# Rotating the SSM state on VectorE ahead of its output matmul

## The chip, the core and the metric

One core of a Trainium2 chip runs the whole program: one launch, all inputs and the output in HBM. The metric is the device time of one execution in microseconds (us). Three executions of the kernel before gave 2878.36, 2879.96 and 2882.97 us; their median, 2879.96 us, is the time before.

## The reference, cut to what matters

The program is one block of a trunk: 16 meta tokens and 2048 tokens of width 1024 pass through a token mixer (a state space model beside an mLSTM, each with its gate) and a gated feed-forward part. The change lies in the state space model (SSM) alone. It has 32 groups of 16 channels, and each group has 64 complex states. With real and imaginary parts written apart, the reference computes for each group

```python
bu_re = jnp.einsum('blgh,gph->blgp', u, bb_re)
bu_im = jnp.einsum('blgh,gph->blgp', u, bb_im)
_, _, x_re, x_im = lax.associative_scan(_complex_affine_combine, (a_re, a_im, bu_re, bu_im), axis=1)
y = (jnp.einsum('blgp,ghp->blgh', x_re, c_re) - jnp.einsum('blgp,ghp->blgh', x_im, c_im) + d * u)
```

that is, a linear recurrence x[t] = a x[t-1] + B u[t] with complex a, and the output y = Re(C x) + d u. The sequence is 2064 tokens long.

## The kernel before, in words

**The SSM by chunks of eight tokens.** The kernel cuts the 2064 tokens into 258 chunks of 8 (the 258 columns of most of its tiles; `C8` in the code). For one group, the inputs of a chunk (8 tokens by 16 channels) stand on the 128 partitions of a tile `ug`, one column per chunk. A first matmul with the weights `wi` gives `vp`: what a chunk adds to the state, 64 real parts on the upper partitions and 64 imaginary parts on the lower ones. Between chunks the state would be multiplied by a complex number a^8. The kernel turns the state by its angle instead, so that the recurrence becomes real: it multiplies `vp` by a rotation (cosines `cc`, sines `ss`, made per group on VectorE from small tables `et`), scans with the real factor `R8` (one `tensor_tensor_scan`, giving `xr`, the state in the turned frame), and has to turn the result back. The output of a group then has three parts, summed in one accumulator `yp` in PSUM: the direct response within a chunk, `tt` times `ug`, and the response to the state at the chunk's start.

**How the turning back is done before.** The turned-back state would be `xr*cc` minus the half-swapped `xr` times `ss` (imaginary and real halves changed over). The kernel never forms that. It forms `xc = xr*cc` (L418) and `xs = xr*ss` (L419) on VectorE, and gives each a matmul with its own weights: `w1` for `xc` (L422) and `w2` for `xs` (L423), where `w2` has the halves changed over and the sign already in it. Both weights are made once, in a stage ahead: for each of 8 blocks of four groups a loop (L797) runs `comb` twice, three VectorE operations each (L790, L791, L792), over a `W1` buffer of which there is one, and writes the result to scratch in HBM (`wo1_d` and `wo2_d`, L800). `load_blk` reads them back for a block of four groups (L378).

**What runs beside it.** All inputs of TensorE here are fp32. The dense projections of the block are matmuls that are split into three products of a rounded part and a rest (L156, L157, L158, 410 columns each, 8 x 3 of them for one tile of a projection). VectorE takes each finished tile out of PSUM (`ev`, L351), ScalarE applies a tanh to it (L352), SyncE sends it to HBM (`gab_d`, `o_d`). There are two buffers of the kind `mm` in PSUM for these tiles, four of the kind `ac`, which the SSM uses. In the SSM's stage ScalarE also copies `vp` into `vs` with its halves changed over (L405, L406), and copies `yp` to `yo` (L425), which goes to HBM.

**What sets the order.** The code is written in stages: projections for the SSM, its preparation, the SSM, then the gates' projections, and so on. A scheduler reorders all of it before the program is built: it goes by priorities in the order of writing, but takes any instruction that its own timing model holds to be ready. So the gates' projections, written after the SSM, are laid between its instructions. What comes out is one fixed list for each engine; on the chip every engine works its list in order and waits at an instruction until what it needs is there. An edit in the SSM can therefore move instructions anywhere after it.

Of the kernel before, what the change touches and what calls it, by code (L numbers as in the profile page):

```python
# [9 lines left out]
F32 = mybir.dt.float32  # L10
F32R = mybir.dt.float32r
I32 = mybir.dt.int32
AF = mybir.ActivationFunctionType
ALU = mybir.AluOpType
# [12 lines left out]
C8 = 258  # L27
# [22 lines left out]
def mixer_ffn_kernel(  # L50
# [7 lines left out]
    stop=None,  # L58
):
    nc = tc.nc  # L60
    S, V, G, P, T = nc.scalar, nc.vector, nc.gpsimd, nc.sync, nc.tensor
# [9 lines left out]
    dp = pool(ctx, "scratch", space=DRAM)  # L71
# [12 lines left out]
    win_d = dp.tile([8, 128, 512], F32, name="win_d")  # L84
    tt_d = dp.tile([8, 128, 512], F32, name="tt_d")
    wo1_d = dp.tile([8, 128, 512], F32, name="wo1_d")
    wo2_d = dp.tile([8, 128, 512], F32, name="wo2_d")
    e_d = dp.tile([8, 128, 4 * 66], F32, name="e_d")

    const = pool(ctx, "const")  # L90
# [279 lines left out]
    def ssm(pl):  # L370
        def load_blk(blk):
            wi = pl.tile([128, 4, 128], F32, tag="wi", name="wi")
            tt = pl.tile([128, 4, 128], F32, tag="tt", name="tt")
            w1 = pl.tile([128, 4, 128], F32, tag="w1", name="w1")
            w2 = pl.tile([128, 4, 128], F32, tag="w2", name="w2")
            et = pl.tile([128, 4, 66], F32, tag="et", name="et", bufs=2)
            for dst, src in ((wi, win_d), (tt, tt_d), (w1, wo1_d), (w2, wo2_d)):
                P.dma_start(out=dst.rearrange("p g c -> p (g c)"), in_=src[blk])  # L378
            P.dma_start(out=et.rearrange("p g a -> p (g a)"), in_=e_d[blk])
            ug = pl.tile([128, 4, C8], F32, tag="ug", name="ug", bufs=2)  # L380
            P.dma_start(out=ug, in_=u_d[blk * 4:blk * 4 + 4].rearrange("g j h c -> (j h) g c"))
            return wi, tt, w1, w2, et, ug

        nxt = load_blk(0)
        for blk in range(8):
            wi, tt, w1, w2, et, ug = nxt
            for g in range(4):
                cc = pl.tile([128, 17, 16], F32, tag="cc", name="cc", bufs=2)
                ss = pl.tile([128, 17, 16], F32, tag="ss", name="ss", bufs=2)
                tb = pl.tile([128, 17, 16], F32, tag="tb", name="tb")  # L390
                shp = [128, 17, 16]
                e2 = lambda o: et[:, g, o:o + 16].unsqueeze(1).to_broadcast(shp)
                e1 = lambda o: et[:, g, o + 16:o + 33].unsqueeze(2).to_broadcast(shp)
                V.tensor_tensor(cc, e1(0), e2(0), ALU.mult)
                V.tensor_tensor(tb, e1(33), e2(33), ALU.mult)
                V.tensor_tensor(cc, cc, tb, ALU.subtract)
                V.tensor_tensor(ss, e1(33), e2(0), ALU.mult)
                V.tensor_tensor(tb, e1(0), e2(33), ALU.mult)
                V.tensor_tensor(ss, ss, tb, ALU.add)
                ccf = cc.rearrange("p a b -> p (a b)")  # L400
                ssf = ss.rearrange("p a b -> p (a b)")
                vp = pst("ac", [128, C8])
                T.matmul(out=vp, lhsT=wi[:, g, :], rhs=ug[:, g, :])
                vs = pl.tile([128, C8], F32, tag="vs", name="vs")
                S.activation(vs[0:64], vp[64:128], AF.Copy)  # L405
                S.activation(vs[64:128], vp[0:64], AF.Copy)  # L406
                a1 = pl.tile([128, C8], F32, tag="a1", name="a1", bufs=2)
                V.tensor_tensor(a1, vp, ccf[:, :C8], ALU.mult)
                V.tensor_tensor(vs, vs, ssf[:, :C8], ALU.mult)
                V.tensor_tensor(a1, a1, vs, ALU.add)  # L410
                xr = pl.tile([128, C8], F32, tag="xr", name="xr")
                V.tensor_tensor_scan(xr, R8[:, blk * 4 + g:blk * 4 + g + 1].to_broadcast([128, C8]), a1, 0.0,
                                     ALU.mult, ALU.add)
                xc = pl.tile([128, C8], F32, tag="xc", name="xc", bufs=2)
                xs = pl.tile([128, C8], F32, tag="xs", name="xs", bufs=2)
                V.memset(xc[:, 0:1], 0.0)
                V.memset(xs[:, 0:1], 0.0)
                V.tensor_tensor(xc[:, 1:C8], xr[:, 0:C8 - 1], ccf[:, 0:C8 - 1], ALU.mult)  # L418
                V.tensor_tensor(xs[:, 1:C8], xr[:, 0:C8 - 1], ssf[:, 0:C8 - 1], ALU.mult)  # L419
                yp = pst("ac", [128, C8])  # L420
                T.matmul(out=yp, lhsT=tt[:, g, :], rhs=ug[:, g, :], start=True, stop=False)
                T.matmul(out=yp, lhsT=w1[:, g, :], rhs=xc, start=False, stop=False)  # L422
                T.matmul(out=yp, lhsT=w2[:, g, :], rhs=xs, start=False, stop=True)  # L423
                yo = pl.tile([128, C8], F32, tag="yo", name="yo", bufs=3)
                S.activation(yo, yp, AF.Copy)  # L425
                P.dma_start(out=ys_d[blk * 4 + g].rearrange("h j c -> (h j) c"), in_=yo)
            if blk < 7:
                nxt = load_blk(blk + 1)
# [121 lines left out]
    with ExitStack() as phG:  # L550
# [52 lines left out]
        for h in range(4):  # L603
# [12 lines left out]
                 rhs=r2f[:, 0:2].rearrange("p a c -> p (a c)"))  # L616
# [29 lines left out]
    with ExitStack() as phS:  # L646
# [12 lines left out]
        nsg = sp.tile([128, 1], F32, name="nsg")  # L659
# [58 lines left out]
        sw = pool(phS, "sprep2")  # L718
# [32 lines left out]
        def big(nm, tag):  # L751
            return sw.tile([128, 32, 16], F32, tag=tag, name=nm)
# [8 lines left out]
        w1 = big("w1", "x2")  # L761
        V.tensor_tensor(bs, Bs, bc(zre), ALU.mult)
        V.tensor_tensor(w1, Bt, bc(zim), ALU.mult)
        V.tensor_tensor(bs, bs, w1, ALU.subtract)
        CA, CA2 = big("CA", "x0"), big("CA2", "x1")
        V.tensor_scalar(CA, Ct, sg, None, ALU.mult)
        V.tensor_scalar(CA2, Cs, nsg, None, ALU.mult)

        shf = sw.tile([128, 240], F32, name="shf")
        V.memset(shf, 0.0)  # L770
# [7 lines left out]
        for blk in range(8):  # L778
# [3 lines left out]
            def pw(a, j0):  # L782
                return a[:, gs, j0:j0 + 8].unsqueeze(3).to_broadcast(shp)

            def col(a):
                return a[:, gs, :].unsqueeze(2).to_broadcast(shp)

            def comb(dst, pa, ca, pb, cb, eng):
                tmp = sw.tile(shp, F32, tag="cmb", name="cmb")
                eng.tensor_tensor(dst, pa, ca, ALU.mult)  # L790
                eng.tensor_tensor(tmp, pb, cb, ALU.mult)  # L791
                eng.tensor_tensor(dst, dst, tmp, ALU.subtract)  # L792

            WB = sw.tile(shp, F32, tag="WB", name="WB")
            comb(WB, pw(Pcr, 0), col(bb), pw(Psr, 0), col(bs), V)
            for ca, cb, dst in ((CA, Cs, wo1_d), (CA2, Ct, wo2_d)):

                W1 = sw.tile([128, 4, 16, 8], F32, tag="W1", name="W1")
                comb(W1.rearrange("p g h j -> p g j h"), pw(Pc, 1), col(ca), pw(Ps, 1), col(cb), V)
                P.dma_start(out=dst[blk], in_=W1.rearrange("p g h j -> p (g h j)"))  # L800
            tpw = pst("tp", [128, 4, 128])
            kp = pst("ac", [128, 4, 16])
            for g in range(4):
# [570 lines left out]
```

## Time and profile before

| quantity | value |
|---|---|
| median of three executions | 2879.96 us |
| the profiled execution | 2886.44 us, of which the span from first to last instruction is 2884.7 us |
| TensorE granted clock | 0.99 of full speed |
| TensorE matmuls, busy | 2794.8 us, 97% of the span |
| TensorE weight loads, busy | 2506.7 us, 87% |
| VectorE (DVE), busy | 1798.8 us, 62% |
| ScalarE (ACT), busy | 1047.4 us, 36% |

In the profile PE is TensorE's matmuls, PEld its weight loads, DVE is VectorE, ACT ScalarE, POOL GpSimd and SP SyncE, which issues the DMAs. A row of a grouped view reads: line, engine, operation, output and inputs, shape, how often; then the busy time in us with the mean of one in ns; then the idle time of the engine ahead of such instructions and what ended it. A row of a view by stretches reads: the stretch, its length, and for each engine its busy time with its number of instructions; then the granted clock and the DMA's share. A row of the timeline reads: start in us, duration in us, engine, line, operation. One fp32 matmul is two instructions in the trace. The weights of the SSM are prepared from about 240 to 320 us of the span, and the SSM itself runs from about 320 to 492 us.

### The profile page before, as it was taken

How to read it: one execution, taken by the hardware profiler on the slowest of the kernel's cores; microseconds unless marked ns; L12 is line 12 of the kernel's file. 1: busy time of each engine (PE TensorE's matmuls, PEld its weight loads, DVE VectorE, ACT ScalarE, POOL GpSimd, SP SyncE). 2: the span in 40 equal slices, each digit the busy share in tenths (PEclk: the TensorE clock that was granted, in tenths of full speed). 3: DMA queues.
4: the chain of work that ended last, by engine and by line, in shares of the span. 5: the costliest groups of instructions: out<-in, count | busy, mean ns of one | idle time of the engine just before them, and what ended most of it. 6: DMA issues, size and time to landing. Idle time of an engine off the chain costs nothing.

```text
span 2884.7 us, 41374 instructions
## 1 busy us (share of the span) xinstructions
PE 2794.8 (97%) x15654; PEld 2506.7 (87%) x15654; DVE 1798.8 (62%) x3508; ACT 1047.4 (36%) x1995; POOL 183.2 (6%) x257
## 2 busy tenths in 40 slices
PE   8999999999999999998779999998999999999999
PEld 8999999999999987776579999996888888888887
DVE  4638897377555465576777777788777774224333
ACT  6102233233443444434344444444444443223221
POOL 1000000000000000212310000001000000000000
PEclk9999999999999999999989999999999999999999
DMA  8334453211454564676746222224222235334553
GB/s 303 105 73 137 169 162 117 74 69 70 147 158 134 159 200 134 196 221 219 234 142 201 80 81 84 71 82 175 81 84 78 87 98 179 95 99 146 166 168 125
DMA packets 328442, 389.74 MB, mean 135 GB/s; under 512 B 41569, under 2 KB 230390, under 8 KB 328114
## 3 DMA queue, kind: packets, MB, share of 16 engines
q1 hardware_dynamic: 328242, 387.10, 41.9%
q8 instruction: 123, 2.02, 0.3%
q14 instruction: 77, 0.63, 0.1%
HBM read 282.90 MB, written 104.12 MB: 134 GB/s over the span
## 4 chain that ended last, share of the span: by engine, by line
PE 83%; DMA 7%; DVE 6%; issue 2%; ACT 1%; POOL 1%; SPq 0%; POOLq 0%; DVEq 0%; ACTq 0%
PE mm L158 9%; PE mm L156 9%; PE mm L157 9%; PE ac L157 8%; PE ac L158 8%; PE ac L156 8%; PE ac L162 5%; PE ac L163 5%; PE ac L161 5%; PE mm L163 4%; PE mm L162 4%; PE mm L161 4%; DMA mk<-h_d 1%; DMA wo_d<-W 1%; DMA h_d<-mk 1%
## 5 line engine op out<-in xcount | busy, mean ns | idle before, releaser
L158 PE MATMUL mm<-hTh,wl 128*128 128x410 f32 (+3 forms) x1216 | 430.4, 354 | 0.0
L156 PE MATMUL mm<-hTh,wh 128*128 128x410 f32 (+3 forms) x1216 | 429.4, 353 | 0.1
L157 PE MATMUL mm<-hTl,wh 128*128 128x410 f32 (+3 forms) x1216 | 427.2, 351 | 0.0
L1275 DVE TENSOR_TENSOR yhl<-ys,yhl 128x1024 fp32r<-128x1024 f32 (+1 forms) x96 | 109.1, 1137 | 293.7 <-ACT yhl L1274 293.7
L157 PE MATMUL ac<-t,yhl 128*128 128x512 f32 x704 | 278.5, 396 | 0.0
L158 PE MATMUL ac<-t,yhl 128*128 128x512 f32 x704 | 277.3, 394 | 0.0
L156 PE MATMUL ac<-t,yhl 128*128 128x512 f32 x704 | 276.6, 393 | 0.0
L161 PE MATMUL mm<-t,w 128*128 128x258 f32 (+2 forms) x792 | 254.6, 322 | 12.6 <-ACT w L1142 9.7
L161 PE MATMUL ac<-t,w 128*128 128x258 f32 (+2 forms) x792 | 255.0, 322 | 12.1 <-ACT t L1047 8.0
L162 PE MATMUL mm<-t,w 128*128 128x258 f32 (+2 forms) x792 | 255.1, 322 | 1.3 <-DVE t L1048 1.3
L162 PE MATMUL ac<-t,w 128*128 128x258 f32 (+2 forms) x792 | 254.9, 322 | 1.1 <-DVE t L1048 1.1
L163 PE MATMUL mm<-t,w 128*128 128x258 f32 (+2 forms) x792 | 253.6, 322 | 1.7 <-DVE w L1143 1.7
L163 PE MATMUL ac<-t,w 128*128 128x258 f32 (+2 forms) x792 | 254.7, 322 | 0.0
L140 ACT ACTIVATE wh<-ws 128x512 fp32r<-128x512 f32 (+1 forms) x176 | 124.5, 708 | 317.7 <-PE mm L157 139.3
L156 PEld LDWEIGHTS mm<-hTh,wh 128*128 128x128 f32 x1216 | 229.2, 188 | 3.2 <-DVE ev L351 0.8
L157 PEld LDWEIGHTS mm<-hTl,wh 128*128 128x128 f32 x1216 | 229.2, 189 | 2.6
L158 PEld LDWEIGHTS mm<-hTh,wl 128*128 128x128 f32 x1216 | 229.2, 189 | 2.4
L1274 ACT ACTIVATE yhl<-ys 128x1024 fp32r<-128x1024 f32 (+1 forms) x96 | 94.8, 988 | 350.6 <-PE ac L157 349.0
L1142 ACT ACTIVATE w<-s 128x512 fp32r<-128x512 f32 x176 | 110.3, 630 | 192.5 <-PE ac L163 112.3
L161 PEld LDWEIGHTS mm<-t,w 128*128 128x128 f32 x792 | 151.0, 191 | 25.6 <-ACT w L1142 9.9
L161 PEld LDWEIGHTS ac<-t,w 128*128 128x128 f32 x792 | 150.7, 190 | 25.1 <-ACT t L1047 8.3
L142 DVE TENSOR_TENSOR wl<-ws,wh 128x512 fp32r<-128x512 f32 (+1 forms) x112 | 104.5, 936 | 108.4 <-ACT wh L140 108.1
(448 smaller groups left out, 6180.2 us busy)
## 6 DMA issues: line engine op xcount, KB each, us to landing
ys<-y_d SPq DMA_DIRECT2D x64, 512.0 KB, 3.7
wg<-in_w_gate_dram SPq DMA_DIRECT2D x44, 512.0 KB, 4.8
wu<-in_w_up_dram SPq DMA_DIRECT2D x44, 512.0 KB, 3.9
gab_d<-ev SPq DMA_DIRECT2D x80, 205.0 KB, 2.2
ws<-in_w_m_dram SPq DMA_DIRECT2D x32, 512.0 KB, 4.0
ws<-in_w_out_dram SPq DMA_DIRECT2D x64, 256.0 KB, 3.0
gat<-gab_d SPq DMA_DIRECT2D x48, 256.0 KB, 3.6
ys<-y_d SPq DMA_DIRECT2D x32, 384.0 KB, 3.1
```

The source lines that it names most:

```text
L140: S.activation(wh, ws, AF.Copy, scale=scale)
L142: V.tensor_tensor(wl, ws, wh.bitcast(F32), ALU.subtract)
L156: T.matmul(out=ps, lhsT=lh, rhs=rh, start=first, stop=False)
L157: T.matmul(out=ps, lhsT=lh, rhs=rl, start=False, stop=False)
L158: T.matmul(out=ps, lhsT=ll, rhs=rh, start=False, stop=last)
L161: T.matmul(out=ps, lhsT=lh, rhs=rh, start=first, stop=False, skip_group_check=True)
L162: T.matmul(out=ps, lhsT=lh, rhs=rl, start=False, stop=False, skip_group_check=True)
L163: T.matmul(out=ps, lhsT=ll, rhs=rh, start=False, stop=last, skip_group_check=True)
L1142: S.activation(t[:, 0], src, AF.Copy)
L1274: S.activation(yh, ys, AF.Copy)
L1275: V.tensor_tensor(yl, ys, yh.bitcast(F32), ALU.subtract)
```

## The change

VectorE forms the turned-back state, and one matmul takes it. `xs` becomes the half-swapped `xr`, copied by ScalarE in two instructions of 64 partitions each; VectorE multiplies it by `ss` in place, and subtracts it from `xc` in place. The matmul with `w2` goes, and with it everything that made and carried `w2`: `CA2`, the second `comb` of each block, the scratch `wo2_d`, its write and its read, and the `memset` of the first column of `xs`. The line numbers of the changed kernel differ by up to 3 from the ones before.

```diff
-            for dst, src in ((wi, win_d), (tt, tt_d), (w1, wo1_d), (w2, wo2_d)):
+            for dst, src in ((wi, win_d), (tt, tt_d), (w1, wo1_d)):
...
                 V.memset(xc[:, 0:1], 0.0)
-                V.memset(xs[:, 0:1], 0.0)
                 V.tensor_tensor(xc[:, 1:C8], xr[:, 0:C8 - 1], ccf[:, 0:C8 - 1], ALU.mult)
-                V.tensor_tensor(xs[:, 1:C8], xr[:, 0:C8 - 1], ssf[:, 0:C8 - 1], ALU.mult)
+                S.activation(xs[0:64, 1:C8], xr[64:128, 0:C8 - 1], AF.Copy)
+                S.activation(xs[64:128, 1:C8], xr[0:64, 0:C8 - 1], AF.Copy)
+                V.tensor_tensor(xs[:, 1:C8], xs[:, 1:C8], ssf[:, 0:C8 - 1], ALU.mult)
+                V.tensor_tensor(xc[:, 1:C8], xc[:, 1:C8], xs[:, 1:C8], ALU.subtract)
                 yp = pst("ac", [128, C8])
                 T.matmul(out=yp, lhsT=tt[:, g, :], rhs=ug[:, g, :], start=True, stop=False)
-                T.matmul(out=yp, lhsT=w1[:, g, :], rhs=xc, start=False, stop=False)
-                T.matmul(out=yp, lhsT=w2[:, g, :], rhs=xs, start=False, stop=True)
+                T.matmul(out=yp, lhsT=w1[:, g, :], rhs=xc, start=False, stop=True)
...
-        V.tensor_scalar(CA2, Cs, nsg, None, ALU.mult)
...
-            for ca, cb, dst in ((CA, Cs, wo1_d), (CA2, Ct, wo2_d)):
-
-                W1 = sw.tile([128, 4, 16, 8], F32, tag="W1", name="W1")
-                comb(W1.rearrange("p g h j -> p g j h"), pw(Pc, 1), col(ca), pw(Ps, 1), col(cb), V)
-                P.dma_start(out=dst[blk], in_=W1.rearrange("p g h j -> p (g h j)"))
+
+            W1 = sw.tile([128, 4, 16, 8], F32, tag="W1", name="W1")
+            comb(W1.rearrange("p g h j -> p g j h"), pw(Pc, 1), col(CA), pw(Ps, 1), col(Cs), V)
+            P.dma_start(out=wo1_d[blk], in_=W1.rearrange("p g h j -> p (g h j)"))
```

Since the scheduler lays all engines' lists anew, the change moves more than it edits. Two places in the built order show it. On VectorE, in the middle of the SSM, before (one group from its scan, L412, to the next group's start; `xc` is L418, `xs` L419, `cc`, `ss` and `tb` make the next group's rotation, `ev` takes a projection tile out of PSUM):

```order
L412 SCALAR_TENSOR_TENSOR xr<-R_2223,a_3416 128x258
L399 TENSOR_TENSOR ss<-ss,tb 128x272
L351 TENSOR_TENSOR ev<-mm,rb 128x410
L418 TENSOR_TENSOR xc<-xr,cc 128x257
L419 TENSOR_TENSOR xs<-xr,ss 128x257
L395 TENSOR_TENSOR tb<-et 128x272
```

and the same place with the change (the scan is now L410, `xc` L415, the product with the swapped half L418, the difference L419):

```order
L410 SCALAR_TENSOR_TENSOR xr<-R_2222,a_3371 128x258
L397 TENSOR_TENSOR ss<-ss,tb 128x272
L350 TENSOR_TENSOR ev<-mm,rb 128x410
L415 TENSOR_TENSOR xc<-xr,cc 128x257
L393 TENSOR_TENSOR tb<-et 128x272
L418 TENSOR_TENSOR xs<-xs,ss 128x257
L392 TENSOR_TENSOR cc<-et 128x272
L419 TENSOR_TENSOR xc<-xc,xs 128x257
```

Four instructions stand between the scan and the product that needs ScalarE's copies, where before the second use of `xr` followed the first at once. Over all 32 groups this number is three or more in 29, and 2, 1 and 2 in the others.

On TensorE, around a group's output matmuls in the same stretch (L156 to L158 are a gate's projection), before:

```order
L156 MATMUL mm<-hTh,wh 128x410
L422 MATMUL ac<-xc,w_3326 128x258
L423 MATMUL ac<-xs,w_3327 128x258
L157 MATMUL mm<-hTl,wh 128x410
L158 MATMUL mm<-hTh,wl 128x410
```

and with the change (the projection is L155 to L157 there):

```order
L157 MATMUL mm<-hTh,wl 128x410
L422 MATMUL ac<-xc,w_3281 128x258
L155 MATMUL mm<-hTh,wh 128x410
L156 MATMUL mm<-hTl,wh 128x410
L157 MATMUL mm<-hTh,wl 128x410
```

The second matmul is gone, and the scheduler spreads the groups wider: from the first group's `vp` matmul to the last one's there are 542 projection matmuls before and 695 with the change. In the stage ahead, from the first block's transposes to the last block's matmuls, there are 269 before and 205 with the change, since that stage has become shorter in the scheduler's model. The lists also differ again far behind, where the feed-forward part begins (about 1480 to 1600 us of the span): there the same instructions stand in a slightly different order.

More of the change, by code (lines that the diff above doesn't have):

```diff
@@ L86, in mixer_ffn_kernel @@
     wo1_d = dp.tile([8, 128, 512], F32, name="wo1_d")
-    wo2_d = dp.tile([8, 128, 512], F32, name="wo2_d")
     e_d = dp.tile([8, 128, 4 * 66], F32, name="e_d")
@@ L374, in load_blk @@
             w1 = pl.tile([128, 4, 128], F32, tag="w1", name="w1")
-            w2 = pl.tile([128, 4, 128], F32, tag="w2", name="w2")
             et = pl.tile([128, 4, 66], F32, tag="et", name="et", bufs=2)
-            for dst, src in ((wi, win_d), (tt, tt_d), (w1, wo1_d), (w2, wo2_d)):
+            for dst, src in ((wi, win_d), (tt, tt_d), (w1, wo1_d)):
                 P.dma_start(out=dst.rearrange("p g c -> p (g c)"), in_=src[blk])
@@ L381, in load_blk @@
             P.dma_start(out=ug, in_=u_d[blk * 4:blk * 4 + 4].rearrange("g j h c -> (j h) g c"))
-            return wi, tt, w1, w2, et, ug
+            return wi, tt, w1, et, ug
         nxt = load_blk(0)
         for blk in range(8):
-            wi, tt, w1, w2, et, ug = nxt
+            wi, tt, w1, et, ug = nxt
             for g in range(4):
@@ L764, in mixer_ffn_kernel @@
         V.tensor_tensor(bs, bs, w1, ALU.subtract)
-        CA, CA2 = big("CA", "x0"), big("CA2", "x1")
+        CA = big("CA", "x0")
         V.tensor_scalar(CA, Ct, sg, None, ALU.mult)
-        V.tensor_scalar(CA2, Cs, nsg, None, ALU.mult)
         shf = sw.tile([128, 240], F32, name="shf")
```

## The prediction

> **What bounds the kernel now.** I read the chain of waits first, then the waits of TensorE, then a view by stretches around the SSM, then the groups of instructions of its steady part.
>
> ```profile
> PE 83%; DMA 7%; DVE 6%; issue 2%; ACT 1%; POOL 1%; SPq 0%; POOLq 0%; DVEq 0%; ACTq 0%
> 240.00:320.00 80.00, 75.41 (x466) 72.33 (x465) 66.58 (x93) 19.16 (x40) 0.00 (x0) 1.00 0.44 158
> 340.00:480.00 140.00, 140.00 (x714) 133.30 (x713) 138.89 (x411) 48.22 (x110) 0.00 (x0) 1.00 0.50 152
> 504.00:576.00 72.00, 72.00 (x385) 71.60 (x385) 25.75 (x39) 15.68 (x24) 1.47 (x5) 1.00 0.21 69
> ```
>
> The chain that ends last is TensorE's for 83%. The columns of the other rows are PE, PEld, DVE, ACT, POOL. In the SSM's steady part (340 to 480 us) TensorE never idles at full clock, and VectorE is full too, 138.89 of 140 us. Just behind the SSM (504 to 576) TensorE is still full, while VectorE has two thirds of its time free: the projections go on. So the SSM runs in the background of a full TensorE, and what leaves TensorE's list there leaves the time. Only in the preparation (240 to 320) does TensorE idle, 80 - 75.41 = 4.6 us, by these waits:
>
> ```profile
> PE tp L805 <- DVE WB L792: 2.6, 2, 1.6
> PE ac L819 <- DVE ks L812: 1.4, 2, 0.9
> PE tp L805 <- ACT ev L352: 0.5, 1, 0.5
> ```
>
> They add up to 4.5 us, 4.0 of it VectorE being late.
>
> **What a removed matmul is worth.** 32 matmuls with `w2` go, two instructions each.
>
> ```profile
> L158 PE MATMUL mm<-hTh,wl 128*128 128x410 f32 x163 | 62.0, 380 | 0.0
> L156 PE MATMUL mm<-hTh,wh 128*128 128x410 f32 x164 | 61.2, 373 | 0.0
> L157 PE MATMUL mm<-hTl,wh 128*128 128x410 f32 x163 | 60.5, 371 | 0.0
> L423 PE MATMUL ac<-xs,w 128*128 128x258 f32 x56 | 16.7, 380 | 0.0
> ...
> 397.63 0.37 PEld L422 LDWEIGHTS ac<-xc,w 128*128 128x128 f32 x2
> 398.03 0.41 PEld L421 LDWEIGHTS ac<-ug,tt 128*128 128x128 f32 x2
> 398.46 0.41 PEld L423 LDWEIGHTS ac<-xs,w 128*128 128x128 f32 x2
> 398.89 0.19 PEld L158 LDWEIGHTS mm<-hTh,wl 128*128 128x128 f32 x1
> ...
> L423 PEld LDWEIGHTS ac<-xs,w 128*128 128x128 f32 x56 | 10.6, 189 | 1.4
> ```
>
> The mean of one instruction, 380 ns, is not its price. 64 x 0.380 would be 24.3 us, but the busy times of these groups (three projection rows, and four SSM matmuls of 16.7 us each) sum to 250 us in a stretch of 140: the instructions overlap. The price is the step from one to the next. The fence shows it for one group: 398.03, 398.46, 398.89, so 0.43 us for a matmul of two instructions. Over the stretch: 163 + 164 + 163 = 490 projection instructions and 4 x 56 = 224 of the SSM make 714, as the row by stretches says. Behind the SSM 385 instructions, nearly all projections, fill 72 us, 0.187 us each. So 140 - 490 x 0.187 = 48.4 us for 224, 0.216 us each. Removing 64 takes **13.8 us** from TensorE.
>
> The Trainium skill, "Perfetto Trace Analysis", section "Identifying the Most-Contended Engine", says that matmul busy time misleads because matmuls are pipelined, and that weight-load busy time is the better measure. The trace agrees on the first half. By the weight loads (one of these lasts 189 ns in the grouped view, and 64 of them 12.1 us) the sum would be 1.7 us smaller, and the forecast that much later; the measured steps decide for 13.8.
>
> **The preparation.** One `comb` of three operations goes from each of 8 blocks, with `CA2`:
>
> ```profile
> L792 DVE TENSOR_TENSOR W<-W,cmb 128x512 f32<-128x512 f32 x16 | 18.8, 1174 | 0.3
> L790 DVE TENSOR_TENSOR W<-Pc,CA 128x512 f32<-128x512 f32 x16 | 18.3, 1145 | 8.3 <-DMA wo_d<-W 8.3
> L791 DVE TENSOR_TENSOR cmb<-Ps,Ct 128x512 f32<-128x512 f32 x8 | 5.5, 690 | 0.2
> L767 DVE TENSOR_SCALAR CA<-Cs,nsg 128x512 f32<-128x512 f32 x1 | 0.5, 483 | 0.0
> ```
>
> 8 x (1.174 + 1.145 + 0.690) + 0.5 = 24.6 us of VectorE's work goes, and most of the 8.3 us that it waited for the one `W1` buffer to be written out, because that buffer is now used once per block and not twice. VectorE is what made TensorE late here. The gain lies between 0 (TensorE's list there has 64 projection matmuls fewer, so the stage is tighter for it too) and the whole 4.6 us. I take **3.5 us**, nearer the upper end, because 4.0 of the 4.5 us waited for VectorE, which loses a third of its 66.58 us. The 16 DMAs of 256 KB that go were beside other work, and I give them nothing.
>
> **The SSM on VectorE and ScalarE.** Here the change adds. Per group VectorE gains one tensor operation and loses a memset; ScalarE gains two copies; and a new wait arises, VectorE's product on ScalarE's copies.
>
> ```profile
> L412 DVE TENSOR_TENSOR_SCAN xr<-R,a 128x258 f32<-128x258 f32 x28 | 19.4, 692 | 0.1
> L351 DVE TENSOR_TENSOR ev<-mm,rb 128x410 f32<-128x410 f32 x21 | 12.2, 579 | 0.0
> L419 DVE TENSOR_TENSOR xs<-xr,ss 128x257 f32<-128x257 f32 x28 | 11.8, 423 | 0.0
> L142 DVE TENSOR_TENSOR wl<-ws,wh 128x1024 fp32r<-128x1024 f32 x5 | 6.1, 1221 | 0.0
> ...
> 399.29 0.42 DVE L409 TENSOR_TENSOR vs<-vs,ss 128x258 f32<-128x258 f32 x1
> 399.63 0.44 DVE L397 TENSOR_TENSOR ss<-et 128x272 f32<-128x272 f32 x1
> 399.99 0.44 DVE L396 TENSOR_TENSOR cc<-cc,tb 128x272 f32<-128x272 f32 x1
> 401.04 0.69 DVE L412 TENSOR_TENSOR_SCAN xr<-R,a 128x258 f32<-128x258 f32 x1
> 401.65 0.42 DVE L399 TENSOR_TENSOR ss<-ss,tb 128x272 f32<-128x272 f32 x1
> 401.98 0.58 DVE L351 TENSOR_TENSOR ev<-mm,rb 128x410 f32<-128x410 f32 x1
> 402.48 0.42 DVE L418 TENSOR_TENSOR xc<-xr,cc 128x257 f32<-128x257 f32 x1
> 406.29 0.60 PE L422 MATMUL ac<-xc,w 128*128 128x258 f32 x2
> ```
>
> VectorE's operations overlap too: the steps are about 0.345 us for a tensor operation (399.29, 399.63, 399.99), 0.61 for the scan, 0.50 for `ev`. A group before is 11 tensor operations, the scan, and its share of `ev` (21 in 28 groups) and of the weights' split L142 (5 in 28, about 1.15 each): 3.80 + 0.61 + 0.38 + 0.21 = 5.0 us. The trace has 28 groups in 140 us, 5.0 each. So VectorE, not TensorE alone, paces the groups now. With the change a group is 12 tensor operations, and the built order has 29 `ev` and 5 splits in 31 groups: 4.14 + 0.61 + 0.47 + 0.19 = 5.4 us, 167 us for 31 groups. TensorE's list between the same two points has 695 projection matmuls and 92 of the SSM with two instructions each: 695 x 0.187 + 184 x 0.216 = 170 us. VectorE still fits under TensorE, by some **2.6 us** in the whole stage, if it never waits. If it falls behind, the projections wait too, since `ev` stands in the same list and there are two `mm` buffers; and the matmul with `xc` waits. Before, that matmul came 406.29 - 402.90 = 3.4 us after its `xc` was done, and I take that for the slack with the change as well. Together 6.0 us of lateness cost TensorE nothing.
>
> The Trainium skill, "VectorE: DVE Perf Modes", section "The DRAIN you can't avoid", says that the next operation does not start until the pipe is empty. By it the added operation would cost its whole 423 ns, 31 x 0.08 = 2.4 us more in the stage, and the 2.6 us would be gone, though TensorE would still not wait. The trace differs: 0.34 us from start to start at 0.42 us each, and the same page says that an operation which nothing holds starts earlier.
>
> Does VectorE wait for the copies? The copies from SBUF are not in the trace of before. The nearest rows:
>
> ```profile
> L406 ACT ACTIVATE vs<-ac 64x258 f32<-64x258 f32 x28 | 10.6, 379 | 0.3
> L352 ACT ACTIVATE ev<-ev 128x410 f32<-128x410 f32 x21 | 11.5, 547 | 34.9 <-DVE ev L351 34.7
> L140 ACT ACTIVATE wh<-ws 128x1024 fp32r<-128x1024 f32 x5 | 5.3, 1062 | 5.7 <-PE mm L157 5.6
> ...
> 395.46 0.58 DVE L351 TENSOR_TENSOR ev<-mm,rb 128x410 f32<-128x410 f32 x1
> 396.08 0.55 ACT L352 ACTIVATE ev<-ev 128x410 f32<-128x410 f32 x1 [2.03 <-DVE ev L351]
> ...
> ACT yo L425 <- PE ac L423: 35.0, 21, 3.4
> ```
>
> From PSUM such a copy takes 0.379 us. From SBUF the slope between 410 and 1024 columns, 0.515 us over 614, puts 257 columns at 0.42, which I take. The scan lasts 0.08 us beyond its step; with some 0.04 us for each signal between engines (the tanh at 396.08 us starts 0.04 after its `ev`, 395.46 + 0.58, ended) the copies are in at 0.08 + 0.04 + 2 x 0.42 + 0.04 = 1.0 us behind the scan's step. Three tensor operations cover 1.03 us, and 29 of 32 groups have three or more there; the other three lose about 0.3, 0.65 and 0.15 us. That is 1.1 us, well under 6.0: **0 us**, as long as ScalarE is free when the scan ends. It has 48.22 of 140 us busy, and gains 28 x 0.84 = 24.
>
> **The sum.** 13.8 + 3.5 = 17.3 us, 0.6%. The profiled execution takes 2886.44 us (span 2884.7), so one like it would take 2869.1; it lies 6.5 us above the median of the three, and the forecast for the median is 2879.96 - 17.3 = **2863 us**.
>
> **Rivals.**
> *VectorE falls behind a little* (0.14). It is full now and will be fuller, and ScalarE works its list in order: a copy can stand behind a `yo` that waits for TensorE. At 0.5 us lost per group, 32 x 0.5 - 6.0 = 10 us come back: 2873; at 0.7 there is no gain: 2879. Against it: ScalarE's waits at `yo`, up to 3.4 us, are for matmuls that the new list puts well ahead of the scan.
> *VectorE falls behind wholly, and the kernel is slower* (0.09). If the copies start late in every group, by as much as the tensor operations between cover, the whole 1.0 us of the trip is exposed at L418 of the changed kernel: 32 x 1.0 - 6.0 = 26 us, 2889. It decides from 0.9 us per group on (slower by 0.2%).
> *The gain is given back later* (0.09). The lists differ again at 1480 to 1600 us, where TensorE idles now:
>
> ```profile
> 1480.00:1520.00 40.00, 32.05 (x247) 31.76 (x248) 35.84 (x66) 19.39 (x34) 8.65 (x5) 0.84 0.46 153
> 1520.00:1560.00 40.00, 36.18 (x301) 35.36 (x300) 30.23 (x62) 15.64 (x29) 2.57 (x6) 1.00 0.55 163
> ```
>
> 11.8 us of idle time, at a granted clock of 0.84 in the first. Another order there can lengthen it or shorten it; a change by as much again would give 2875 one way and 2851 the other. I see no row that says which.
> *The busy time is the price* (0.06). If each of the 64 instructions really costs 0.380 us and the preparation gives all 4.6, the time is 2880 - 28.9 = 2851. Against it stands the overlap above.
> That the second matmul stays in some form is excluded by the built order.
>
> **Chances and range.** The forecast has 0.62; its own range is 2859 to 2867 (0 to 4.6 us from the preparation, 0.21 to 0.22 us per instruction). What a measurement of this kernel can tell is about 0.2%, 5.8 us: faster means under 2874.2, slower over 2885.7. Faster: 0.60 of the forecast's 0.62, 0.05 of a little behind, 0.07 of given back later, 0.06 of the busy price, 0.78. Slower: 0.09. The rest, 0.13, within. The range reaches from the busy price to a little behind without gain: 2852 to 2878.
>
> **What would show it.** Right: in the SSM no waits of TensorE on `xc`, groups every 5.4 to 5.5 us, steady parts with TensorE full; in the preparation under 2 us of TensorE idle; 64 matmul instructions fewer; the idle time behind 1200 us unchanged within 5 us. Wrong: idle TensorE ahead of the matmul with `xc` or of projections behind `ev`, VectorE waiting for ScalarE at the product in most groups, or copies well above 0.42 us.

## The result, and the profile after

The changed kernel takes **2862.68 us** (median of four executions, 2861.60 to 2864.68), beside 2879.94 us for the kernel before in the same comparison: a ratio of 0.994, 95% interval 0.9922 to 0.9957, that is 17.3 us less (12 to 22). Timed again in a second comparison it took 2867.43 us against 2882.03, a ratio of 0.9945 (0.9933 to 0.9956). The forecast was 2863 us. The total came out as forecast, but one term of its sum did not, as the stages show.

The view by stretches of the kernel after, over three of the stretches shown of before (columns: stretch, length, PE, PEld, DVE, ACT, POOL, granted clock, DMA share, GB/s):

```profile
240.00:320.00 80.00, 80.00 (x492) 79.21 (x492) 57.83 (x104) 24.21 (x52) 0.00 (x0) 1.00 0.45 157
340.00:480.00 140.00, 140.00 (x725) 135.36 (x724) 138.06 (x382) 67.64 (x157) 0.10 (x1) 1.00 0.42 136
504.00:576.00 72.00, 72.00 (x385) 71.58 (x384) 36.82 (x58) 19.37 (x29) 2.85 (x10) 1.00 0.19 67
```

TensorE's idle time in the preparation is gone (80.00 of 80 us busy, before 75.41), and the view of waits holds none for TensorE from 216 to 520 us. From the last `ut` to the first `buf`, two events that are explained below, TensorE has 1831 instructions where it had 1895: the 64 that were to go are gone. VectorE is still full in the SSM (138.06 of 140), and TensorE still never waits for it.

The groups of the changed steps, from 220 to 505 us of the same kernel:

```profile
L422 PE MATMUL ac<-xc,w 128*128 128x258 f32 x64 | 19.1, 381 | 0.0
L418 DVE TENSOR_TENSOR xs<-xs,ss 128x257 f32<-128x257 f32 x32 | 13.5, 422 | 0.5 <-ACT xs L417 0.5
L419 DVE TENSOR_TENSOR xc<-xc,xs 128x257 f32<-128x257 f32 x32 | 13.5, 422 | 0.1
L416 ACT ACTIVATE xs<-xr 64x257 f32<-64x257 f32 x32 | 13.4, 418 | 27.0 <-DVE xr L410 26.6
L417 ACT ACTIVATE xs<-xr 64x257 f32<-64x257 f32 x32 | 13.4, 418 | 0.4
L788 DVE TENSOR_TENSOR W<-Pc,CA 128x512 f32<-128x512 f32 x8 | 9.4, 1170 | 7.6 <-DMA wo_d<-W 7.6
```

The matmul with `xc` never waits. A copy from SBUF takes 418 ns, as the prediction had it (0.42). VectorE waited for a copy once, 0.5 us in all. ScalarE stands ready at the first copy and waits for the scan (26.6 us), which is the right way round. VectorE still waits 7.6 us for the `W1` buffer to be written out (8.3 before).

Where the time went is read best from two events that both kernels have: the last of the twelve copies of the SSM's input projections out of PSUM (`ut`), and the first of the forty copies that the part behind begins with (`buf`). Between them lie the preparation, the SSM and the gates' projections. A row of a view by tile gives the count, the duration in ns (least, median, most), and the first and last start. Before:

```profile
L361 DVE TENSOR_TENSOR ut<-mm,rb x12: 814/837/866, 122.6 to 199.6; 128x344 f32<-128x344 f32 x12
L439 DVE TENSOR_TENSOR buf<-mm,rb x40: 586/587/593, 553.9 to 730.1; 128x412 f32<-128x412 f32 x24, 128x414 f32<-128x414 f32 x16
```

After:

```profile
L360 DVE TENSOR_TENSOR ut<-mm,rb x12: 798/828/866, 120.7 to 198.2; 128x344 f32<-128x344 f32 x12
L438 DVE TENSOR_TENSOR buf<-mm,rb x40: 586/587/593, 532.3 to 708.5; 128x412 f32<-128x412 f32 x24, 128x414 f32<-128x414 f32 x16
```

The stage between them took 553.9 - 199.6 = 354.3 us and now takes 532.3 - 198.2 = 334.1: **20.2 us less**. Behind the first `buf` these two profiles take the same, 2884.7 - 553.9 = 2330.8 and 2862.9 - 532.3 = 2330.6 us.

One point on counting instructions, since the price of a matmul hangs on it. The text ahead calls all inputs of TensorE fp32. In the code the projections' inputs (`hTh`, `hTl`, `wh`, `wl`) are stored as `float32r`, a rounded form, and one of their matmuls is one instruction in the trace (24 for a finished tile); the SSM's matmuls are fp32 and two instructions each. The prediction counted them so.

### The profile page after: what moved, and what is told of

It is laid out like the page before. It is cut to its first block, busy times and chain, and to the rows that moved or that the text cites. A ratio compares the mean times of both kernels' runs of the same rounds, so it can differ in the third digit from the quotient of the medians.

```text
span 2862.9 us, 41241 instructions
## 1 busy us (share of the span) xinstructions
PE 2778.0 (97%) x15590; PEld 2495.6 (87%) x15590; DVE 1782.9 (62%) x3483; ACT 1068.3 (37%) x2059; POOL 182.6 (6%) x257
## 5 line engine op out<-in xcount | busy, mean ns | idle before, releaser
L157 PE MATMUL mm<-hTh,wl 128*128 128x410 f32 (+3 forms) x1216 | 428.5, 352 | 0.0
L155 PE MATMUL mm<-hTh,wh 128*128 128x410 f32 (+3 forms) x1216 | 428.2, 352 | 0.0
L156 PE MATMUL mm<-hTl,wh 128*128 128x410 f32 (+3 forms) x1216 | 427.9, 352 | 0.0
L156 PE MATMUL ac<-t,yhl 128*128 128x512 f32 x704 | 278.7, 396 | 0.0
L157 PE MATMUL ac<-t,yhl 128*128 128x512 f32 x704 | 277.5, 394 | 0.0
L155 PE MATMUL ac<-t,yhl 128*128 128x512 f32 x704 | 276.8, 393 | 0.0
L160 PE MATMUL ac<-t,w 128*128 128x258 f32 (+2 forms) x792 | 256.0, 324 | 12.1 <-ACT t L1044 8.0
L156 PEld LDWEIGHTS mm<-hTl,wh 128*128 128x128 f32 x1216 | 229.0, 188 | 2.5
L157 PEld LDWEIGHTS mm<-hTh,wl 128*128 128x128 f32 x1216 | 229.1, 188 | 2.2
L155 PEld LDWEIGHTS mm<-hTh,wh 128*128 128x128 f32 x1216 | 229.0, 188 | 2.0
L160 PEld LDWEIGHTS mm<-t,w 128*128 128x128 f32 x792 | 151.2, 191 | 27.9 <-ACT w L1139 9.6
```

The costliest lines, as they stand in the source:

```text
L155: T.matmul(out=ps, lhsT=lh, rhs=rh, start=first, stop=False)
L156: T.matmul(out=ps, lhsT=lh, rhs=rl, start=False, stop=False)
L157: T.matmul(out=ps, lhsT=ll, rhs=rh, start=False, stop=last)
L160: T.matmul(out=ps, lhsT=lh, rhs=rh, start=first, stop=False, skip_group_check=True)
```

## Experiments

All are told by the same events. "Stage" is from the last `ut` to the first `buf`, "behind" from there to the end of the span. Of the last three rows and of twelve added operations there is one execution each, the profiled one. Each ratio is to the kernel before as it was timed beside that run: 2879.94 us for the first two rows, 2882.28 for both preparations kept, one preparation, three state matmuls and four added operations, 2882.03 for the second comparison, no cover and the merged matmuls. Times from different comparisons are therefore best set side by side by their ratios.

| kernel | time, us | ratio to before | last `ut` | first `buf` | stage | behind |
|---|---|---|---|---|---|---|
| before | 2879.94 | 1 | 199.6 | 553.9 | 354.3 | 2330.8 |
| after | 2862.68 | 0.994 (0.9922 to 0.9957) | 198.2 | 532.3 | 334.1 | 2330.6 |
| after, second comparison | 2867.43 | 0.9945 (0.9933 to 0.9956) | 198.3 | 532.4 | 334.1 | 2334.1 |
| both preparations kept | 2873.03 | 0.9965 (0.9953 to 0.9977) | 198.7 | 539.2 | 340.5 | 2333.0 |
| before with one preparation | 2875.59 | 0.997 (0.9959 to 0.9981) | 198.9 | 547.1 | 348.2 | 2327.2 |
| three state matmuls | 2887.97 | 1.0024 (1.0015 to 1.0032) | 198.8 | 560.8 | 362.0 | 2325.9 |
| four added VectorE operations | 2869.54 | 0.9952 (0.994 to 0.9965) | 200.2 | 536.5 | 336.3 | 2331.8 |
| no cover for the copies | 2871.91 | 0.9956 (0.9942 to 0.9971) | 198.0 | 538.2 | 340.2 | 2331.5 |
| twelve added operations | 2962.98 | one execution | 198.5 | 635.6 | 437.1 | 2325.6 |
| merged preparation matmuls | 2861.34 | 0.9922 (0.9909 to 0.9936) | 197.8 | 530.2 | 332.4 | 2325.4 |
| before, second profile | 2887.06 | one execution | 199.3 | 553.8 | 354.5 | 2331.4 |
| after, third profile | 2865.60 | one execution | 197.4 | 531.5 | 334.1 | 2332.3 |
| before, third profile | 2885.12 | one execution | 199.7 | 553.6 | 353.9 | 2329.7 |

The stage repeats within 0.6 us from one profile of a kernel to the next. The part behind, which no edit touches, ranges from 2325.4 to 2334.1 us, so a few us are told apart by the stage and not by the total.

In three runs (four and twelve added operations, no cover) the SSM ends so late that the list lays matmuls of the next part ahead of its end. Their stage then holds, on balance, 12, 22 and 20 TensorE instructions more than after's 1831, which belong to the part behind. For these the last of the forty `buf` copies is the fairer end: up to it TensorE has 2766 or 2767 instructions, as after has (2766). From the last `ut` to there it is 510.3 us after, and 512.6, 612.0 and 514.2 us in the three: 2.3, 101.7 and 3.9 us more.

### One part of the change alone, from each side

*The matmul alone.* The changed kernel, with the second weights still made and written out, though nothing reads them:

```diff
+        V.tensor_scalar(CA2, Cs, nsg, None, ALU.mult)
...
-            W1 = sw.tile([128, 4, 16, 8], F32, tag="W1", name="W1")
-            comb(..., pw(Pc, 1), col(CA), pw(Ps, 1), col(Cs), V)
-            P.dma_start(out=wo1_d[blk], in_=...)
+            for ca, cb, dst in ((CA, Cs, wo1_d), (CA2, Ct, wo2_d)):
+                W1 = sw.tile([128, 4, 16, 8], F32, tag="W1", name="W1")
+                comb(..., pw(Pc, 1), col(ca), pw(Ps, 1), col(cb), V)
+                P.dma_start(out=dst[blk], in_=...)
```

> The changed kernel, but the weights of the removed matmul are still made on VectorE and written to HBM (and never read). Theory of the forecast (TensorE sets the time, 13.8 us of the gain are the removed matmuls, up to 4.6 us the preparation): 2863 + 4 = 2867 us, with 4 to 5 us of TensorE idle back in the preparation. Rival (the gain is VectorE's relief in the preparation, 24.6 us of work there): most of the gain is gone, 2875 to 2880 us.

```profile
L439 DVE TENSOR_TENSOR buf<-mm,rb x40: 585/587/593, 539.2 to 715.5; 128x412 f32<-128x412 f32 x24, 128x414 f32<-128x414 f32 x16
```

Measured: 2873.03 us, between the two forecasts and 6 us above the first (before took 2.3 us more beside this run than beside the first of after). The stage tells more: 539.2 - 198.7 = 340.5 us. It is 13.8 us shorter than before, which is what is left of the change here, and 6.4 us longer than after, which is what keeping the preparation costs. Its weight loads by line, from 220 to 340 us, show the stalls that came back:

```profile
L819 PEld LDWEIGHTS ac<-ks,shf 128*128 128x128 f32 x64 | 7.6, 191 | 0.9 <-DVE ks L812 0.8
L805 PEld LDWEIGHTS tp<-ident,WB 128*128 128x128 f32 x32 | 6.5, 203 | 4.1 <-DVE WB L792 3.5 <-ACT ev L352 0.6
```

They are 5.0 us. In one stretch of this run (280 to 300 us) the granted clock was 0.92 besides; by an estimate from that number it cost up to 0.08 x 20 = 1.6 us.

*The preparation alone.* The kernel before, both matmuls kept; the second weights are not made, and the first are loaded in their place, so the state's part of the output is another:

```diff
-            for dst, src in ((wi, win_d), (tt, tt_d), (w1, wo1_d), (w2, wo2_d)):
+            for dst, src in ((wi, win_d), (tt, tt_d), (w1, wo1_d), (w2, wo1_d)):
...
-            for ca, cb, dst in ((CA, Cs, wo1_d), (CA2, Ct, wo2_d)):
+            for ca, cb, dst in ((CA, Cs, wo1_d),):
```

> The kernel before, with both matmuls per group, but the second set of weights is not made: the second matmul takes the first one's weights again, so the output of the state space model is not the reference's. Theory of the forecast: only the preparation's part is gained, 2880 - 4 = 2876 us, TensorE idle in the preparation near 0. Rival (VectorE's relief is the gain): about 2863 us.

The first and last of the `buf` copies here, and TensorE's stage (first two columns behind the length: PE and PEld) before and here:

```profile
L438 DVE TENSOR_TENSOR buf<-mm,rb x40: 585/587/593, 547.1 to 723.3; 128x412 f32<-128x412 f32 x24, 128x414 f32<-128x414 f32 x16
199.60:553.90 354.30, 349.71 (x1895) 338.00 (x1894) 268.78 (x676) 92.22 (x196) 4.64 (x9) 1.00 0.42 134
198.90:547.10 348.20, 348.18 (x1895) 338.85 (x1894) 246.19 (x651) 91.28 (x196) 4.63 (x9) 1.00 0.40 130
```

Measured: 2875.59 us, where 2876 was forecast. The stage is 348.2 us, **6.1 us** under before with the same 1895 instructions of TensorE, and TensorE has no wait from 216 to 520 us. The other 14.1 us of the stage's gain are the SSM's. So from both sides the preparation is worth 6.1 to 6.4 us and the matmuls 13.8 to 14.1, and they add up to the 20.2. The preparation's figure lies above the upper bound of 4.6 us that the prediction gave it.

Why the bound was low is most likely in a row that the prediction did not read: the idle time of the weight loads, from 220 to 505 us. Before:

```profile
L819 PEld LDWEIGHTS ac<-ks,shf 128*128 128x128 f32 x64 | 7.5, 192 | 2.2 <-DVE ks L812 2.0
L805 PEld LDWEIGHTS tp<-ident,WB 128*128 128x128 f32 x32 | 6.5, 203 | 4.3 <-DVE WB L792 3.1 <-ACT ev L352 1.2
```

After, the same two lines, from 220 to 340 us:

```profile
L816 PEld LDWEIGHTS ac<-ks,shf 128*128 128x128 f32 x64 | 7.8, 192 | 0.0
L802 PEld LDWEIGHTS tp<-ident,WB 128*128 128x128 f32 x32 | 6.5, 204 | 0.0
```

By the weight loads TensorE stood idle 2.2 + 4.3 = 6.5 us at those two lines, by the matmuls' busy time 4.5. A matmul is shown busy for some 380 ns where the step to the next is 190 to 216, so the tail of the last one before a stall probably covers the first part of it. The measured 6.1 to 6.4 us stand with the weight loads. The Trainium skill, "Perfetto Trace Analysis", section "Identifying the Most-Contended Engine", holds weight-load busy time to be a better measure than matmul busy time of how near TensorE is to its roofline. For the idle time of this stage the trace agrees (6.5 against 6.1 to 6.4 measured); of the price of one matmul, which comes next, that section says nothing.

### The price of one matmul

The changed kernel with the state's matmul made three times per group, into the same accumulator, so that the state's part counts three times in the output: 64 matmuls, or 128 instructions, more.

```diff
-                T.matmul(out=yp, lhsT=w1[:, g, :], rhs=xc, start=False, stop=True)
+                for i in range(3):
+                    T.matmul(out=yp, lhsT=w1[:, g, :], rhs=xc, start=False, stop=i == 2)
```

> The changed kernel with the matmul on the turned-back state made three times per group (the state's part of the output counts threefold, so it is not the reference's): 64 matmuls more, 128 instructions. Price by the step, 0.216 us per instruction: 2863 + 27.7 = 2891 us. Price by the weight loads' busy time, 0.189: 2887 us. Price by the matmuls' busy time, 0.380: 2912 us.

```profile
L439 DVE TENSOR_TENSOR buf<-mm,rb x40: 586/588/592, 560.8 to 737.0; 128x412 f32<-128x412 f32 x24, 128x414 f32<-128x414 f32 x16
```

Measured: a stage of 362.0 us, 27.9 more than after: 27.9 / 128 = **0.218 us** per instruction, where the prediction had 0.216. By the weight loads' 0.189 us it would have been 24.2, by the busy mean of 0.380 us 48.6. The total, 2887.97 us, lies between the first two forecasts and tells them apart badly, because the part behind happened to be 2325.9 us here; the stage tells them apart.

### How much room VectorE has

Four, and then twelve, multiplications of 258 columns were added to each group on VectorE, into a tile that nothing reads:

```diff
+                jx = pl.tile([128, C8], F32, tag="jx", name="jx")
+                for i in range(4):
+                    V.tensor_tensor(jx, a1, ccf[:, :C8], ALU.mult)
```

> The changed kernel with four more tensor operations of 258 columns on VectorE in each group (their result is not used). 32 x 4 x 0.345 = 44 us more of VectorE's work in a stage where it is already full. Theory of the forecast, carried on (the state space model is a background of TensorE's projections, and the scheduler lays more of them between the groups, 947 in place of 695 from the first group to the last): no change, 2861 to 2866 us, groups every 6.8 to 7.0 us, TensorE full. Rival (VectorE paces the stage and with it the time): 2863 + 44 - 3 = 2904 us.

The scan's row of after, then of four added operations, and there the `buf` copies, a late stretch and TensorE's only wait between 216 and 640 us:

```profile
L410 DVE TENSOR_TENSOR_SCAN xr<-R,a x32: 683/689/700, 311.8 to 480.7; 128x258 f32<-128x258 f32 x32
```

```profile
L410 DVE TENSOR_TENSOR_SCAN xr<-R,a x32: 678/686/695, 313.9 to 533.5; 128x258 f32<-128x258 f32 x32
L441 DVE TENSOR_TENSOR buf<-mm,rb x40: 580/587/593, 536.5 to 712.8; 128x412 f32<-128x412 f32 x24, 128x414 f32<-128x414 f32 x16
504.00:560.00 56.00, 53.90 (x283) 52.51 (x282) 46.76 (x114) 19.71 (x40) 1.28 (x6) 1.00 0.23 74
PE mm L155 <- DVE buf L441: 2.1, 1, 2.1
```

After: (480.7 - 311.8) / 31 = 5.45 us per group. With four operations more: (533.5 - 313.9) / 31 = 7.08, so the SSM takes 219.6 us in place of 168.9, 50.7 longer. Up to the last `buf` the kernel lost only 2.3 us, and TensorE was full until the SSM's end; its one wait, 2.1 us, lies behind it. The total is 2869.54 us, 3.5 us above the forecast range of 2861 to 2866 and far from the rival's 2904; both of after's ratios, 0.994 and 0.9945, lie in the interval of this run's (0.994 to 0.9965). In the scheduler's list 947 projection matmuls now stand between the first group and the last, where the change alone has 695: the room is not the few us by which VectorE's list is shorter than TensorE's, but all projections that are left to be laid between. After the change 532.3 - 480.7 = 51.6 us of them are still to come when the last scan starts.

> The changed kernel with twelve more tensor operations of 258 columns on VectorE in each group (result not used). VectorE needs 31 x (5.4 + 12 x 0.345) = 296 us for the stage; TensorE's list has 948 projection matmuls of the gates and 48 of the next part between the first group and the last, 996 x 0.187 + 40 = 226 us. Theory (the groups are free only while projections are left): about 70 us of TensorE idle at the end of the stage, 2863 + 70 = 2933 us. If the stage stayed hidden: 2866 us.

With twelve added operations the scan's row, its first twenty and last eleven scans alone, the matmul's wait and three stretches read:

```profile
L410 DVE TENSOR_TENSOR_SCAN xr<-R,a x32: 686/692/699, 312.3 to 626.5; 128x258 f32<-128x258 f32 x32
L410 DVE TENSOR_TENSOR_SCAN xr<-R,a x20: 686/692/699, 312.3 to 518.1; 128x258 f32<-128x258 f32 x20
L410 DVE TENSOR_TENSOR_SCAN xr<-R,a x11: 687/694/695, 536.9 to 626.5; 128x258 f32<-128x258 f32 x11
PE ac L425 <- DVE xc L419: 54.4, 12, 7.2
340.00:480.00 140.00, 140.00 (x737) 137.38 (x736) 134.40 (x363) 45.05 (x96) 0.00 (x0) 1.00 0.33 106
560.00:600.00 40.00, 16.64 (x28) 6.51 (x26) 39.73 (x117) 7.92 (x20) 0.00 (x0) 0.50 0.15 42
600.00:640.00 40.00, 12.38 (x25) 7.18 (x26) 38.99 (x105) 8.52 (x20) 0.47 (x3) 0.50 0.05 15
```

Here the slower side shows: 2962.98 us. Until 480 us TensorE is full as ever. Then the projections have run out, VectorE alone sets the pace (39.73 of 40 us), and the matmul with `xc` waits 54.4 us in twelve waits. The SSM is 314.2 - 168.9 = 145.3 us longer and the time to the last `buf` 101.7, so 44 us were covered. The forecast of 2933 us came out 30 us low: a group took 314.2 / 31 = 10.14 us where 9.54 was expected, 19 us over all groups. Half of that is work that the list put there: 40 `ev` and 8 splits of weights between the first and the last scan, where the forecast had after's 29 and 5. By the steps that makes 24 x 0.345 + 0.61 + 0.65 + 0.30 = 9.84 us a group; the other 0.3 us are VectorE's own waits, 9.7 us in all. The remaining 11 of the 30 us were not taken apart.

### The copies without cover

The changed kernel with one more order given to the scheduler: each group's VectorE instructions stand behind the difference of the group before. Only the product `xc` is then left between the scan and the product that needs the copies.

```diff
+                with (tc.issue_after(last.ins) if last else ExitStack()):
...
-                V.tensor_tensor(xc[:, 1:C8], xc[:, 1:C8], xs[:, 1:C8], ALU.subtract)
+                    last = V.tensor_tensor(xc[:, 1:C8], xc[:, 1:C8], xs[:, 1:C8], ALU.subtract)
```

> The changed kernel, with an ordering edge: VectorE's instructions of a group stand behind the difference of the group ahead, so that only the product with the cosines stands between a scan and the product that needs ScalarE's copies. About 1.0 - 0.35 = 0.65 us of each group is then a wait of VectorE on ScalarE. The prediction's rival (VectorE falls behind wholly): 32 x 0.65 - 6.0 = 15 us back, 2878 us. Theory after the run with four more operations (the scheduler lays out more projections for slower groups, and only their end is a limit): 2863 to 2868 us, with the wait on ScalarE plainly in the trace and TensorE full until the gates' projections are used up.

The scan's row and the `buf` copies, VectorE's wait for the copies in the SSM, TensorE's two waits, and a late stretch:

```profile
L412 DVE TENSOR_TENSOR_SCAN xr<-R,a x32: 684/695/698, 310.8 to 535.7; 128x258 f32<-128x258 f32 x32
L440 DVE TENSOR_TENSOR buf<-mm,rb x40: 580/587/593, 538.2 to 712.2; 128x412 f32<-128x412 f32 x24, 128x414 f32<-128x414 f32 x16
DVE xs L420 <- ACT xs L419: 20.9, 27, 1.1
PE ac L424 <- DVE xc L421: 2.3, 1, 2.3
PE mm L155 <- DVE buf L440: 1.2, 1, 1.2
520.00:560.00 40.00, 36.57 (x191) 35.12 (x190) 30.75 (x63) 14.32 (x27) 1.28 (x6) 1.00 0.19 63
```

The trip is now exposed in most groups (27 waits, 0.77 us each), and with the stricter order a group takes 7.25 us, 1.8 more than after: twice the 0.9 us from which the rival "slower" was to decide. The waits are 0.67 us of the 1.8, and the 40 `ev` and 8 splits that now fall among the groups some 0.3 by their steps; the rest was not taken apart. Up to the last `buf` the kernel lost 3.9 us, not the 56 us by which the SSM is longer, and it is still faster than before (0.9956). The total of 2871.91 us lies between the two forecasts. So the cover that the prediction counted in 29 of 32 groups is real and used, but losing it costs about 4 us, because the projections behind the SSM take up the rest.

### Was anything given back later?

The change was timed again, and both kernels were profiled further:

> The changed kernel, unchanged, beside the next three on the same chip: 2863 us by the forecast, a ratio of 0.994 to the kernel before.

> The kernel before, for one more profile. Three numbers are read from it: the stage from the last of the twelve copies of the SSM's projections out of PSUM to the first of the forty of the next part's (354.3 us in the profile of before, 334.1 in both of after), and the part behind that copy (2330.8 us in the profile of before, 2330.6 and 2334.1 in those of after), which no edit touches. If the stage's 20.2 us reach the end whole, the part behind takes about as long here as with the change, within the scatter of 2325 to 2334 us. If some 3 us of them are given back later, it takes 2327 to 2331 us less 3 to 6, so under 2326.

> The changed kernel, for one more profile beside the other two on the same chip. Both theories: the stage at 334.1 us within 0.5. The part behind it: about as long as in the two profiles of the kernel before, if nothing is given back later; 3 to 6 us longer than those, if it is.

> The kernel before once more, to see its own scatter. Both theories: the stage at 354.3 us within 0.5; the part behind as in the other profile of it, within the scatter that this pair shows.

One of the profiles of before, and one of after:

```profile
L439 DVE TENSOR_TENSOR buf<-mm,rb x40: 586/588/593, 553.6 to 729.8; 128x412 f32<-128x412 f32 x24, 128x414 f32<-128x414 f32 x16
```

```profile
L438 DVE TENSOR_TENSOR buf<-mm,rb x40: 586/587/593, 531.5 to 707.8; 128x412 f32<-128x412 f32 x24, 128x414 f32<-128x414 f32 x16
```

The part behind took 2330.8, 2331.4 and 2329.7 us before (mean 2330.6), and 2330.6, 2334.1 and 2332.3 after (mean 2332.3). That is 1.7 us more, within the spread of after's own three. The sign that the prediction set on it is met too: TensorE's idle time behind 1200 us of the span was 65.7 to 68.8 us in the three profiles of before, and behind the same place, 1178.4 us, 65.3 to 68.8 in those of after. Ahead of the stage the changed kernel is 1.6 us earlier (199.5 to 198.0 on the mean); its variants reach the same point at 197.8 to 200.2, so this may be scatter. The six profiled spans differ by 2884.4 - 2864.4 = 20.0 us on the mean, as the stage alone does. The medians of all executions differ by less, 17.3 and 14.6 us. The profiled executions of before lie above the others timed beside them (2886.44 beside a median of 2879.96, 2887.06 and 2885.12 beside 2884.92), those of after by 2.0 and 0.8 us above their medians. What makes that difference no trace here shows, and it stays open. 20 us lie inside the first interval (12 to 22 us) and just outside the second (13 to 19).

### A version that goes further

In the changed kernel's preparation the transposes and the small matmuls load the same weights `WB`. Each pair was merged into one matmul of 144 columns, the identity beside 16 columns of `CA` that GpSimd copies there:

```diff
...
-                T.transpose(tpw[:, g, :], wbg, ident)
-                T.matmul(out=kp[:, g, :], lhsT=wbg, rhs=CA[:, blk * 4 + g, :])
...
+                    G.tensor_copy(rI[:, gg % 3, 128:144], CA[:, gg, :])
+                    T.matmul(out=tk[:, g, :], lhsT=wbg, rhs=rI[:, gg % 3, :])
...
```

> The changed kernel, and in the preparation the transpose of a group's input weights and the small matmul that loads the same weights become one matmul of 144 columns (identity and 16 columns side by side, copied together by GpSimd): 32 + 64 TensorE instructions become 64. If the step of such an instruction is the weight load, 0.20 us: 32 x 0.20 = 6.4 us less, 2857 us. If the preparation becomes bound by VectorE, GpSimd or ScalarE again (two copies out of PSUM in place of one, and 32 small GpSimd copies ahead of the matmuls), TensorE idles there and nothing is gained: 2863 us or more.

Measured: 2861.34 us, beside 2867.43 for the change in the same comparison: the lowest median of all that were run. But the stage gives only 1.7 us of it; the other 4 to 5 lie in the part behind (2325.4 us), which the edit does not touch and in which lists and runs scatter. The 6.4 us that were expected of the stage did not come. TensorE has no wait in this run from 216 to 640 us, so a new wait, the other forecast, is not the cause. The weight loads in the timeline (start, duration, engine, line) show it. One block of the changed kernel, in its second run (first and last rows of the block, and the row behind it):

```profile
238.66 0.14 PEld L802 LDWEIGHTS tp<-ident,WB 128*128 128x128 f32 x1
238.85 0.30 PEld L803 LDWEIGHTS ac<-CA,WB 128*128 128x128 f32 x2
...
239.67 0.34 PEld L803 LDWEIGHTS ac<-CA,WB 128*128 128x128 f32 x2
239.93 0.19 PEld L155 LDWEIGHTS mm<-hTh,wh 128*128 128x128 f32 x1
```

and of the merged one, where the list puts six of a block's eight instructions together and two later, with projections between:

```profile
238.17 0.86 PEld L810 LDWEIGHTS tp<-rI,WB 128*128 128x128 f32 x6
238.97 0.19 PEld L155 LDWEIGHTS mm<-hTh,wh 128*128 128x128 f32 x1
...
242.27 0.37 PEld L810 LDWEIGHTS tp<-rI,WB 128*128 128x128 f32 x2
242.58 0.19 PEld L155 LDWEIGHTS mm<-hTh,wh 128*128 128x128 f32 x1
```

Twelve small instructions took 239.93 - 238.66 = 1.27 us, 0.106 each, and not the 0.20 that the expectation took from the mean length of a weight load (204 ns in the row of L802 above). The eight merged ones take 0.80 + 0.31 = 1.11. The gain is 0.16 us a block, 1.3 us for eight blocks, near the measured 1.7.

## Why the prediction was right, and where it was not

**What bounds the stage: right.** TensorE is full through the SSM, and what left its list left the time. 32 matmuls were costed at 13.8 us by the steps; the runs gave 13.8 and 14.1, and 0.218 us per instruction when 128 were added. The rival of the busy-time price (24.3 us) is refuted by the same run, and so is the price by the weight loads (12.1 us).

**The preparation: the mis-sized term.** The step "I take 3.5 us", with the bound "the whole 4.6 us", measured 6.1 to 6.4. Its mechanism held, VectorE being late and no longer being late. Its size was read from the matmuls' idle time, which probably hides the start of each stall; the weight loads' idle time at the same two lines, 6.5 us, comes out near what was measured.

**"Most of the 8.3 us that it waited for the one `W1` buffer": wrong, and without effect.** 7.6 us of the wait remain, and TensorE waits nowhere in the preparation all the same.

**VectorE and ScalarE: right in the small.** A group takes 5.45 us (5.4 predicted), a copy 0.418 us (0.42), the added operation its step of about 0.345 us, and VectorE waited for the copies once, 0.5 us in all. The run with four added operations bears the step out: 16 operations a group at 0.345 us, with the scan and the 40 `ev` and 8 splits that the trace has over 31 groups, make 5.52 + 0.61 + 0.65 + 0.30, about 7.1 us, and 7.08 was measured. By the rule of the Trainium skill, "VectorE: DVE Perf Modes", section "The DRAIN you can't avoid", taken without the exception that it names itself, each would cost its whole 0.42 us and the group 1.2 us more; the measurement bears out the exception.

**"Together 6.0 us of lateness cost TensorE nothing": much too small** for lateness that the scheduler knows of. Lengthened by 50.7, 56.0 (535.7 - 310.8 in the run without cover, less 168.9) and 145.3 us, the SSM cost 2.3, 3.9 and 101.7 us up to the last `buf`, so 44 to 52 us were covered each time. That is near the 51.6 us of projections that are left when after's last scan starts; by it alone the three would have cost 0, 4.4 and 93.7 us. The rivals "a little behind" and "wholly behind", both priced on 6.0 us, were priced too high. What a lateness costs that the list does not foresee was not tried.

**Given back later: not seen** beyond 1.7 us, inside the scatter.

**The total** was met in part by luck. The preparation gave 2.6 to 2.9 us more than its 3.5, so the sum that the stage and the profiled executions show is 20 us and not 17.3; the medians of all executions happen to differ by 17.3 and 14.6. The prediction's own range has a slip besides: 0 to 4.6 us and 0.21 to 0.22 us per instruction give 2861 to 2867, not 2859 to 2867.

## What to carry to other kernels

Where TensorE is full, cost a removed matmul by the step from one to the next, and a removed stall by the idle time of its weight loads; in this case the busy time of pipelined matmuls was too high for the first and, as it seems, hid part of the second. Work that runs in the background of another stage has as much room as that stage has work left when it ends, so long as the order is laid anew: read it as the time from the background's last step to the next stage's first. Here that estimate came within 2.3, 0.5 and 8 us of three measured costs. And when an edit is worth 0.5% of a long kernel, measure it between two events that enclose it, since the part that nothing touched may scatter by nearly half as much.

## What the runs showed of the hardware

With TensorE mostly waiting, its granted clock fell by half: 0.50 from 560 to 640 us with twelve added operations, where it was 1.00 in the full stretches. The Trainium skill, "TensorE: Matmul & The Clock Gate", section "Part 1: The HAM clock gate", says that an idle TensorE is put on half its pulses, and the trace agrees. The groups were not slowed by it: the last eleven scans, 536.9 to 626.5 us, all at half the clock, stand 89.6 / 10 = 8.96 us apart, about what VectorE's steps make without `ev` and splits (24 x 0.345 + 0.61 = 8.89), and the first twenty, at full clock, 205.8 / 19 = 10.83.

Small fp32 matmuls are cheaper than their busy means say: transposes of 128 columns and matmuls of 16 columns, shown as 298 and 222 ns long, followed one another every 0.106 us.
